# Moving the accumulations of the modulation vectors in a two-layer hybrid encoder from attention to the output projection and the feed-forward part

## The chip, the cores and the metric

The kernel runs on one core of a Trainium2 chip. The metric is the device time of one execution in microseconds (us), lower is better. Engines are named as in the profile: PE is TensorE (PEld its weight loads), DVE is VectorE, ACT is ScalarE, POOL is GpSimd, SP is SyncE, whose queue issues the transfers.

## The reference, cut to what matters

Two layers work on 256 tokens of 1024 channels in float32. Each layer has an attention part and a feed-forward part, and six modulation vectors of 1024 values that depend only on the conditioning vector `c` and on weights, and not on the tokens:

```
mod = silu(c) @ ada_w + ada_b                      # 1024 x 6144 weights in each layer
sh_m, sc_m, g_m, sh_f, sc_f, g_f = split(mod, 6)   # vectors 0 to 5

h = rms_norm(x, norm_mix_g) * (1 + sc_m) + sh_m    # vectors 1 and 0
proj = h @ w_in                                    # 1024 x 5024
... three attention branches, 4 + 4 + 8 heads ...
merged = sum of sigmoid(gate) * (branch @ w_branch)
x = x + g_m * (merged @ w_out)                     # vector 2

h = rms_norm(x, norm_ffn_g) * (1 + sc_f) + sh_f    # vectors 4 and 3
gate, up = split(h @ ffn_w_gate_up, 2)             # 1024 x 5632
x = x + g_f * ((silu(gate) * up) @ ffn_w_down)     # vector 5; 2816 x 1024
```

## The kernel before

**Items.** All large products are cut into items, in one list for both layers (`items`, 248 of them). An item is 256 rows by up to 512 columns of a weight (512 KB). `load_split` (L241) loads it from SP's queue into a buffer `raw` (five of them, `rawp`), ACT rounds it into `whi` (L187) and DVE takes the remainder into `wlo` (L188); there are seven pairs of these (`spl`). For each of the two blocks of 128 tokens PE then does six matmuls of 512 columns (three products for each 128 rows, L268 to L270). In the main loop the first block's `step` of an item is written down with the item and the second block's four items later (`LAG = 4`), except in the first twelve items, where both stand together. So a pair of `whi` and `wlo` is held from its split until the second block's matmuls.

In layer 0, items 0 to 17 are the first part of the input projection, 18 to 41 the gates, 42 to 49 the branch projections, 50 to 57 the output projection, 58 to 101 the gate and up part of the feed-forward part (`iF` is 58, `iD` is 102), 102 to 123 its down projection. Layer 1 follows with items 124 to 247; its gates are items 142 to 165. Attention has no items of its own: its pieces (scores, softmax, transposes, products) are set beside the items of the gates by `at(i, f)`, which runs `f` ahead of item i's load.

**Modulation vectors.** Vectors 1 and 0 of layer 0 are made ahead of everything (`first_sums`, `first_mod`). Each of the others is made in two halves of four units (`ada_units`, L143). A unit loads 256 x 512 of `ada_w` into one of the same five `raw` buffers from the same queue, and DVE multiplies each of its two slices by a value of silu(c) and adds it to `acc` (L138 for the first slice of a half, L140 for the other seven). After the fourth unit a half is summed over partitions: for vectors 0, 1, 3 and 4 by `col_mod` (four transposes on PE, a reduction and two or three small operations on DVE), for 2 and 5 by two matmuls and an addition. `spread` (L800) sets units at even distances beside a range of items. A unit stands ahead of the load of its item, so in SP's queue and in the ring of five buffers it goes first.

**Order.** The instructions of each engine are put in order at build time by a scheduler that follows the order in which they are written where operands allow; `manual_schedule` keeps PE's order inside a block as written. `later(k, fn)` writes `fn` k steps (a step is one block of an item) later. `na_bias` loads the bias table of the neighbourhood heads and adds the mask to it on DVE (L349). `post_g1` normalizes the low-rank parts; its late part `b_` (L379) transposes them and splits them for `w_uq` and `w_ukv` (items 16 and 17).

Of the kernel before, what the change touches and what calls it, by code (L numbers as in the profile page):

```python
# [12 lines left out]
ALU = mybir.AluOpType  # L13
AX = mybir.AxisListType

P = 128
# [5 lines left out]
W = 64  # L22
# [5 lines left out]
DC = 9  # L28
# [8 lines left out]
def encoder_kernel(ctx: ExitStack, tc: tile.TileContext, x, consts, cols, rows, ada_b, rpb, ada_w, w_in,  # L37
                   w_uq, w_ukv, w_na, w_mla, w_gqa, w_out, w_gu, w_dn, fng, out):
    nc = tc.nc
# [18 lines left out]
    def nm(s):  # L58
        uid[0] += 1
        return f"{s}_{uid[0]}"  # L60
# [4 lines left out]
    def t2(shape, dtype=F32):  # L65
        return tmp.tile(shape, dtype, tag="tm", name=nm("tm"))
# [4 lines left out]
    def tpb():  # L71
        return pstp.tile([P, 512], F32, tag="tp", name=nm("tp"))
# [16 lines left out]
    mask = con[:, o:o + 64]; o += 64  # L89
# [44 lines left out]
    def ada_acc(acc, raw, kc0, nk):  # L134
        for j in range(nk):
            kc = kc0 + j
            if kc == 0:
                nc.vector.tensor_scalar_mul(acc, raw[:, j, :], sc[:, 0:1])  # L138
            else:
                nc.vector.scalar_tensor_tensor(out=acc, in0=raw[:, j, :], scalar=sc[:, kc:kc + 1], in1=acc,  # L140
                                               op0=ALU.mult, op1=ALU.add)

    def ada_units(l, m, hf, row):  # L143
        st = {}

        def unit(u):
            def go():
                if u == 0:
                    st["acc"] = modp.tile([P, 512], F32, tag="acc", name=nm("acc"))
                raw = rawp.tile([P, 2, 512], F32, tag="raw", name=nm("raw"))  # L150
                c0 = m * D + hf * 512
                nc.sync.dma_start(raw, ada_w[l, u * 256:(u + 1) * 256, c0:c0 + 512].rearrange("(k p) n -> p k n", p=P))
                ada_acc(st["acc"], raw, 2 * u, 2)
                if u == 3:
                    fin()
            return go

        def fin():
            acc = st["acc"]
            if not row:  # L160
                later(DG, lambda: col_mod(l, m, hf * 4, 4, acc))
                return
            if hf == 0:
                mods[(l, m)] = modp.tile([P, D], F32, tag="G", name=nm("G"), bufs=1)
            bb = t2([P, 512])
            c0 = m * D + hf * 512
            nc.sync.dma_start(bb, ada_b[l, c0:c0 + 512].partition_broadcast(P))
            ah, al = t2([P, 512], F32R), t2([P, 512], F32R)
            split_to(ah, al, acc)

            def b_():
                ps = tpb()
                nc.tensor.matmul(ps, onesr, ah, start=True, stop=False)
                nc.tensor.matmul(ps, onesr, al, start=False, stop=True)
                nc.vector.tensor_tensor(out=mods[(l, m)][:, hf * 512:(hf + 1) * 512], in0=ps, in1=bb, op=ALU.add)

            later(DG, b_)

        return [unit(u) for u in range(4)]
# [6 lines left out]
    def split_to(hi_ap, lo_ap, src):  # L186
        nc.scalar.copy(hi_ap, src)  # L187
        nc.vector.tensor_tensor(out=lo_ap, in0=src, in1=hi_ap.bitcast(F32), op=ALU.subtract)  # L188
# [99 lines left out]
    def later(k, fn):  # L288
        deferred.append((cur[0] + k, fn))
# [8 lines left out]
    def at(i, fn):  # L298
        side.setdefault(i, []).append(fn)
# [9 lines left out]
    def layer(l):  # L309
# [3 lines left out]
        i0 = len(items)  # L313
# [24 lines left out]
        def na_bias():  # L338
            st["bias"] = []
            for t in range(NT):  # L340
                hk = t4([P, 16, W])
                for r in range(2):
                    base = rpb[l, 2 * t + r]
                    src = bass.AP(tensor=base.tensor, offset=base.offset, ap=[[1, W], [127, 16], [1, W]])
                    nc.sync.dma_start(hk[r * W:(r + 1) * W], src)
                b = t4([P, 16, W])
                rev = bass.AP(tensor=hk.tensor, offset=hk.offset + W - 1, ap=[list(hk.ap[0]), [W, 16], [-1, W]])
                for h in range(4):
                    nc.vector.tensor_tensor(out=b[:, 4 * h:4 * h + 4, :], in0=rev[:, 4 * h:4 * h + 4, :],  # L349
                                            in1=mask.unsqueeze(1).to_broadcast([P, 4, W]), op=ALU.add)  # L350
                st["bias"].append(b)

        def lazy(key, shape):
# [7 lines left out]
        def post_g1(t, ps):  # L361
            c = t2([P, 416])
            nc.scalar.copy(c, ps[:, 0:416])
            junk = t2([P, 512])
            s = sm(2)
            nc.scalar.activation(junk[:, 0:256], c[:, 0:256], AF.Square, scale=1.0 / 16.0, accum_out=s[:, 0:1])
            nc.scalar.activation(junk[:, 256:384], c[:, 256:384], AF.Square, scale=float(128.0 ** -0.5),
                                 accum_out=s[:, 1:2])
            ms = sm(2)
            nc.vector.tensor_scalar_add(ms, s, EPS)  # L370
            r = rstd_of(ms, 2)
            rw = st["rw"]
            cn = t2([P, 384])
            nc.vector.scalar_tensor_tensor(out=cn[:, 0:256], in0=c[:, 0:256], scalar=r[:, 0:1], in1=rw[:, 0:256],
                                           op0=ALU.mult, op1=ALU.mult)
            nc.vector.scalar_tensor_tensor(out=cn[:, 256:384], in0=c[:, 256:384], scalar=r[:, 1:2], in1=rw[:, 256:384],
                                           op0=ALU.mult, op1=ALU.mult)

            def b_():  # L379
                tpt = tpb()  # L380
                tv = tpt.rearrange("p (j q) -> p j q", j=4)
                for j in range(3):
                    nc.tensor.transpose(tv[:, j, :], cn[:, j * P:(j + 1) * P], ident)
                cT = t4([P, 2, 3, P], F32R)
                st.setdefault("cT", {})[t] = cT
                split_to(cT[:, 0], cT[:, 1], tv[:, 0:3, :])
                kr = c[:, 384:416]
                kpe = st["kpe"][:, t, :]
                ab = t2([P, 2, 32])
                a, b = ab[:, 0], ab[:, 1]  # L390
                nc.vector.tensor_tensor(out=a, in0=kr, in1=mlC[:, t, :], op=ALU.mult)
                for h in range(2):
                    nc.vector.tensor_tensor(out=b[:, h * 16:(h + 1) * 16], in0=kr[:, (1 - h) * 16:(2 - h) * 16],
                                            in1=mlS[:, t, h * 16:(h + 1) * 16], op=ALU.mult)
                nc.vector.tensor_tensor(out=kpe, in0=a, in1=b, op=ALU.add)

            later(DC, b_)

        def post_ga(t, ps):
            q = t2([P, 512])  # L400
# [138 lines left out]
        iB = len(items)  # L539
# [110 lines left out]

        flush.add(i0)
        at(i0 + (7 if l == 0 else 0), params)
        at(i0 + (12 if l == 0 else 8), na_bias)


        st["m"] = {}
# [35 lines left out]
        iO = len(items)  # L692
# [107 lines left out]
        def spread(units, a, b):  # L800
            n = len(units)
            for i, f in enumerate(units):
                at(a + (i * (b - a)) // n, f)

        spread([f for m, row in ((2, True), (4, False), (3, False)) for hf in range(2) for f in ada_units(l, m, hf, row)],
               i0 + 24, iB + 4)
        un = [f for hf in range(2) for f in ada_units(l, 5, hf, True)]
        if l + 1 < L:
            un += [f for m in (1, 0) for hf in range(2) for f in ada_units(l + 1, m, hf, False)]
        else:  # L810
            def load_fng():
                f = t4([P, D])
                nc.sync.dma_start(f, fng.partition_broadcast(P))
                state["fng"] = f
            at(iF + 30, load_fng)
# [5 lines left out]
    for l in range(L):  # L821
        layer(l)
    xT0 = {}

    def first_x():
        xT = act.tile([P, KC, S], F32, tag="lo", name=nm("xT"))
# [75 lines left out]
    for i, it in enumerate(items):  # L902
        if i in flush:
            while pend:
                step(1, pend.pop(0))
        if i == 0:
            raws = first_loads(0)
            first_x()
            first_mod(0, first_sums(0, raws))
        for f in side.get(i, ()):  # L910
            f()
        load_split(it)
        if i < 12:

            q1 = i // 3 + 1
            if i % 3 == 1 and q1 < 4:
                raws = first_loads(q1)
            with tc.manual_schedule(engines={mybir.EngineType.PE}):
                if i % 3 == 1 and q1 < 4:
                    four = first_sums(q1, raws)  # L920
                if i % 3 == 2 and q1 < 4:
                    first_mod(q1, four)
                step(0, i)
                step(1, i)
            continue
        if len(pend) >= LAG:
            step(1, pend.pop(0))
        step(0, i)
        pend.append(i)
# [71 lines left out]
```

## Time and profile before

| | |
|---|---|
| median of 3 runs | 822.5 us (822.18 to 823.59) |
| the profiled execution, its own time | 822.51 us |
| its span, from the first to the last instruction | 820.4 us |
| mean granted clock of TensorE | 0.991 |
| PE busy | 790.7 us (96%) |
| DVE busy | 598.8 us (73%) |
| ACT busy | 453.7 us (55%) |
| read from HBM | 185.44 MB, 227 GB/s over the span |

Busy times are unions of the instructions of an engine. PE's matmuls are pipelined, so short waits can hide in its busy time. The 2.1 us by which the execution is longer than its span lie around it.

### The profile page before, as it was taken

What the parts mean: (1) busy time and instruction counts of PE and PEld (TensorE: products, weight loads), DVE (VectorE), ACT (ScalarE), POOL (GpSimd) and SP (SyncE); (2) the same over time, 40 slices, a digit from 0 to 9 for tenths busy, and PEclk for the clock granted to TensorE, in tenths of its full rate; (3) what the DMA queues carried; (4) which work ended last, traced back from release to release, by engine and by line L of the source; (5) the groups of instructions that cost most, each with busy time, mean ns of one, the idle gap of its engine ahead of it and who ended that gap; (6) DMA issues with size and microseconds to landing.
All of it is one profiled execution on the core that took longest, in us unless ns stands there. A gap on an engine that the chain in (4) does not pass through costs nothing.

```text
span 820.4 us, 10803 instructions
## 1 busy us (share of the span) xinstructions
PE 790.7 (96%) x3776; PEld 633.4 (77%) x3776; DVE 598.8 (73%) x955; ACT 453.7 (55%) x788; POOL 25.8 (3%) x40
## 2 busy tenths in 40 slices
PE   5998999999999999999999999999999999999996
PEld 3786776788878888888878877777887888888884
DVE  3369898789777888875667699878978666665462
ACT  4365887644485444443466687774448544444441
POOL 1002100000000000000000020000000000000000
PEclk9999999999999999999999999999999999999998
DMA  9979488697667989886874668778765677876631
GB/s 315 359 245 273 131 293 252 198 311 227 194 180 241 322 294 306 276 264 190 210 213 137 180 192 279 222 230 283 250 198 182 219 233 223 259 226 184 182 103 52
DMA packets 113414, 187.20 MB, mean 228 GB/s; under 512 B 14672, under 2 KB 34256, under 8 KB 113360
## 3 DMA queue, kind: packets, MB, share of 16 engines
q1 hardware_dynamic: 113360, 186.51, 73.1%
q8 instruction: 30, 0.49, 0.3%
q14 instruction: 24, 0.20, 0.1%
HBM read 185.44 MB, written 1.05 MB: 227 GB/s over the span
## 4 chain that ended last, share of the span: by engine, by line
issue 49%; PE 31%; DVE 8%; DMA 6%; ACT 4%; POOL 1%; POOLq 0%; DVEq 0%; ACTq 0%
PE mm L268 8%; PE mm L270 8%; PE mm L269 8%; DMA raw<-in_ada_w_dram 6%; DVE wlo L188 2%; DVE acc L140 2%; PE tp L861 1%; POOL sm L108 1%; PE o L629 1%; ACT P L587 1%; ACT tm L218 1%; DVE sm L574 1%; PE tp L209 1%; PE tp L608 1%; PE tp L560 1%
## 5 line engine op out<-in xcount | busy, mean ns | idle before, releaser
L188 DVE TENSOR_TENSOR wlo<-raw,whi 128x1024 fp32r<-128x1024 f32 (+2 forms) x248 | 298.3, 1209 | 115.0 <-ACT whi L187 114.8
L187 ACT CAST whi<-raw 128x1024 fp32r<-128x1024 f32 (+2 forms) x248 | 256.9, 1041 | 221.6 <-PE mm L270 137.1
L268 PE MATMUL mm<-whi,hi 128*128 128x512 f32 (+1 forms) x784 | 314.0, 400 | 1.8 <-ACT hi L882 1.1
L270 PE MATMUL mm<-whi,lo 128*128 128x512 f32 (+1 forms) x784 | 307.1, 392 | 0.2
L269 PE MATMUL mm<-wlo,hi 128*128 128x512 f32 (+1 forms) x784 | 306.1, 390 | 0.5 <-DVE wlo L188 0.4
L268 PEld LDWEIGHTS mm<-whi,hi 128*128 128x128 f32 x784 | 148.1, 189 | 34.7 <-issue 5.7
L270 PEld LDWEIGHTS mm<-whi,lo 128*128 128x128 f32 x784 | 147.7, 188 | 32.8 <-DVE lo L188 1.8
L269 PEld LDWEIGHTS mm<-wlo,hi 128*128 128x128 f32 x784 | 148.3, 189 | 28.9 <-DVE wlo L188 1.7
L140 DVE SCALAR_TENSOR_TENSOR acc<-raw,sc,acc 128x512 f32<-128x512 f32 x140 | 104.9, 749 | 32.2 <-DMA raw<-in_ada_w_dram 30.5
L270 PE MATMUL mm<-whi,s 128*128 128x512 f32 (+1 forms) x188 | 73.3, 390 | 2.4 <-DVE s L188 2.4
L268 PE MATMUL mm<-whi,s 128*128 128x512 f32 (+1 forms) x188 | 74.2, 395 | 0.4 <-ACT s L187 0.4
L269 PE MATMUL mm<-wlo,s 128*128 128x512 f32 (+1 forms) x188 | 73.1, 389 | 0.0
L270 PEld LDWEIGHTS mm<-whi,s 128*128 128x128 f32 x188 | 35.4, 189 | 9.8 <-DVE s L188 2.6
L268 PEld LDWEIGHTS mm<-whi,s 128*128 128x128 f32 x188 | 35.3, 188 | 7.9 <-ACT s L187 0.9
L269 PEld LDWEIGHTS mm<-wlo,s 128*128 128x128 f32 x188 | 35.4, 188 | 6.8
L592 ACT ACTIVATE P<-P,sm 128x256 f32<-128x256 f32 x64 | 29.3, 509 | 5.7 <-DVE sm L590 5.6
L587 ACT ACTIVATE P<-tp,sm,rq 128x256 f32<-128x256 f32 x32 | 17.8, 561 | 15.9 <-DVE sm L584 15.8
L197 POOL TENSOR_SCALAR sm<-ss 128x1 f32<-128x1 f32 x10 | 4.0, 404 | 662.4 <-ACT tm L192 662.4
L218 ACT ACTIVATE tm<-tp,cm,cm 128x128 f32<-128x128 f32 x48 | 21.3, 472 | 6.2 <-PE tp L209 6.2
L108 POOL TENSOR_TENSOR sm<-sm,nhalf 128x1 f32<-128x1 f32 (+2 forms) x22 | 18.4, 835 | 127.1 <-DVE sm L370 65.2
L192 ACT ACTIVATE tm<-x_sb 128x512 f32<-128x512 f32 x20 | 12.6, 632 | 16.8 <-DVE x_sb L703 14.6
L733 DVE TENSOR_TENSOR tm<-tm,mm 128x512 f32<-128x512 f32 (+1 forms) x24 | 15.4, 640 | 8.7 <-PE mm L270 7.1
(157 smaller groups left out, 637.7 us busy)
## 6 DMA issues: line engine op xcount, KB each, us to landing
raw<-in_ada_w_dram SPq DMA_DIRECT2D x80, 512.0 KB, 4.8
raw<-in_w_gu_dram SPq DMA_DIRECT2D x80, 512.0 KB, 4.6
raw<-in_w_in_dram SPq DMA_DIRECT2D x64, 512.0 KB, 4.6
raw<-in_w_dn_dram SPq DMA_DIRECT2D x44, 512.0 KB, 4.8
s<-in_ada_w_dram SPq DMA_DIRECT2D x32, 256.0 KB, 6.7
raw<-in_w_out_dram SPq DMA_DIRECT2D x16, 512.0 KB, 4.9
raw<-in_w_in_dram SPq DMA_DIRECT2D x16, 256.0 KB, 5.0
raw<-in_w_gqa_dram SPq DMA_DIRECT2D x8, 512.0 KB, 5.6
```

Of the source, the lines that this page charges most:

```text
L108: nc.gpsimd.tensor_tensor(out=r, in0=ms, in1=nhalf[:, 0:n], op=ALU.pow)
L140: nc.vector.scalar_tensor_tensor(out=acc, in0=raw[:, j, :], scalar=sc[:, kc:kc + 1], in1=acc, op0=ALU.mult, op1=ALU.add)
L187: nc.scalar.copy(hi_ap, src)
L188: nc.vector.tensor_tensor(out=lo_ap, in0=src, in1=hi_ap.bitcast(F32), op=ALU.subtract)
L192: nc.scalar.activation(junk, x_sb[:, t, hf * 512:(hf + 1) * 512], AF.Square, scale=1.0 / 32.0, accum_out=ss[:, hf:hf + 1])
L218: nc.scalar.activation(fv[:, j, :], xT[:, j, :], AF.Identity, scale=A[:, kc:kc + 1], bias=B[:, kc:kc + 1])
L268: nc.tensor.matmul(ps[t][:, 0:n], lhs(t, 0, kc), hi[:, j, 0:n], start=first, stop=False)
L269: nc.tensor.matmul(ps[t][:, 0:n], lhs(t, 0, kc), lo[:, j, 0:n], start=False, stop=False)
L270: nc.tensor.matmul(ps[t][:, 0:n], lhs(t, 1, kc), hi[:, j, 0:n], start=False, stop=last)
L587: nc.scalar.activation(pt[:, t, :], src[:, t, :], AF.Exp, bias=nb[:, t:t + 1], scale=scale[t], accum_out=rs[:, t:t + 1])
L592: nc.scalar.activation(pt[:, t, :], pt[:, t, :], AF.Copy, scale=rc[:, t:t + 1])
L733: nc.vector.tensor_tensor(out=hd[:, 0:n], in0=sgv, in1=up, op=ALU.mult)
```

## The change

Of the units, layer 0's vectors 2, 4 and 3 (24 units) are spread over items 24 to 53 and no longer over 24 to 45. Layer 1 keeps only vector 2 (8 units) beside its attention; its vectors 4 and 3 (16 units) go to the feed-forward part of layer 0, whose 34 items 68 to 101 so get 40 units in place of 24, in the order 5, 1, 0, 4, 3. Four smaller edits come with it. The mask is added by one instruction in place of four. `na_bias` of layer 0 stands at item 11 in place of 12. The late part of `post_g1` in layer 0 comes 6 steps after it in place of 9. In the first twelve items each block's PE instructions are put behind the last PE instruction written before them (an edge in PE's own order; nothing waits for a result).

```diff
-                for h in range(4):
-                    nc.vector.tensor_tensor(out=b[:, 4 * h:4 * h + 4, :], in0=rev[:, 4 * h:4 * h + 4, :],
-                                            in1=mask.unsqueeze(1).to_broadcast([P, 4, W]), op=ALU.add)
+                nc.vector.tensor_tensor(out=b, in0=rev, in1=mask.unsqueeze(1).to_broadcast([P, 16, W]), op=ALU.add)
...
-            later(DC, b_)
+            later(6 if l == 0 else DC, b_)
...
-        at(i0 + (12 if l == 0 else 8), na_bias)
+        at(i0 + (11 if l == 0 else 8), na_bias)
...
-        spread([f for m, row in ((2, True), (4, False), (3, False)) for hf in range(2) for f in ada_units(l, m, hf, row)],
-               i0 + 24, iB + 4)
+        ms = ((2, True), (4, False), (3, False)) if l == 0 else ((2, True),)
+        spread([f for m, row in ms for hf in range(2) for f in ada_units(l, m, hf, row)], i0 + 24, iO + 4 if l == 0 else iB + 4)
         un = [f for hf in range(2) for f in ada_units(l, 5, hf, True)]
         if l + 1 < L:
-            un += [f for m in (1, 0) for hf in range(2) for f in ada_units(l + 1, m, hf, False)]
+            un += [f for m in (1, 0, 4, 3) for hf in range(2) for f in ada_units(l + 1, m, hf, False)]
...
+    def last_pe():
+        return next(i for i in reversed(nc.cur_bb.bb.instructions) if i.engine == mybir.EngineType.PE)
...
-            with tc.manual_schedule(engines={mybir.EngineType.PE}):
+            with tc.issue_after(last_pe()), tc.manual_schedule(engines={mybir.EngineType.PE}):
```

## Rows read from the trace of the kernel before

**Rows 1.** The page: busy time, share and instructions of each engine.

```profile
PE 790.7 (96%) x3776; PEld 633.4 (77%) x3776; DVE 598.8 (73%) x955; ACT 453.7 (55%) x788; POOL 25.8 (3%) x40
```

**Rows 2.** Stretches of 20 us: length, busy of each engine, clock, DMA share, GB/s.

```profile
0.00:20.00 20.00, 9.94 (x45) 6.59 (x46) 5.84 (x18) 9.85 (x19) 2.25 (x8) 0.92 0.95 314
...
60.00:80.00 20.00, 16.93 (x79) 13.36 (x78) 18.67 (x50) 12.67 (x23) 5.07 (x5) 0.96 1.00 262
80.00:100.00 20.00, 19.88 (x103) 14.37 (x101) 17.16 (x47) 17.43 (x47) 2.24 (x2) 0.96 0.47 129
...
800.00:820.00 20.00, 12.57 (x56) 10.09 (x54) 4.27 (x6) 2.89 (x6) 1.72 (x4) 0.89 0.14 53
```

**Rows 3.** PE's waits from 60 to 100 us: total, times, longest.

```profile
PE mm L270 <- DVE s L188: 2.4, 1, 2.4
PE mm L268 <- ACT s L187: 0.4, 1, 0.4
```

**Rows 4.** DVE's timeline around that wait: start, duration, instruction.

```profile
62.24 0.35 DVE L376 SCALAR_TENSOR_TENSOR tm<-tm,sm,rw 128x128 f32<-128x128 f32 x1
...
75.20 1.42 DVE L349 TENSOR_TENSOR s<-s,con 128x256 f32<-128x256 f32 x4
76.54 1.01 DVE L188 TENSOR_TENSOR s<-tp,s 128x384 fp32r<-128x384 f32 x2
```

**Rows 5.** PE's timeline: the second block's transposes of `post_g1`.

```profile
66.42 0.49 PE L383 MATMUL tp<-con,tm 128*128 128x128 f32 x3
```

**Rows 6.** Stages of layer 0, columns as in rows 2.

```profile
97.00:160.00 63.00, 61.48 (x319) 45.61 (x318) 51.42 (x89) 47.13 (x107) 0.00 (x0) 1.00 0.78 251
...
182.00:216.00 34.00, 34.00 (x163) 28.17 (x162) 31.91 (x43) 15.20 (x17) 0.00 (x0) 1.00 0.71 220
216.00:234.00 18.00, 17.05 (x80) 13.95 (x79) 12.58 (x15) 10.82 (x19) 1.09 (x2) 1.00 0.67 201
...
258.00:346.00 88.00, 88.00 (x411) 72.84 (x410) 73.46 (x95) 39.08 (x46) 0.00 (x0) 1.00 0.91 305
...
358.00:424.00 66.00, 65.17 (x299) 53.76 (x297) 38.57 (x47) 29.72 (x37) 1.14 (x2) 1.00 0.76 209
```

**Rows 7.** Stages of layer 1: attention, and the gate and up part.

```profile
460.00:560.00 100.00, 97.82 (x516) 75.00 (x515) 85.69 (x159) 74.63 (x163) 5.75 (x5) 1.00 0.74 225
...
650.00:740.00 90.00, 90.00 (x414) 74.45 (x413) 58.43 (x63) 43.13 (x50) 0.00 (x0) 1.00 0.76 236
```

**Rows 8.** ACT's longest waits, 258 to 346 us (layer 0, gate and up).

```profile
ACT whi L187 <- DMA raw<-in_w_gu_dram: 33.8, 19, 3.1
ACT whi L187 <- PE mm L270: 6.0, 4, 3.1
```

**Rows 9.** ACT's longest wait, 650 to 740 us (layer 1, gate and up).

```profile
ACT whi L187 <- PE mm L270: 32.5, 21, 2.1
```

**Rows 10.** All of DVE's waits, 258 to 346 us.

```profile
DVE acc L140 <- DMA raw<-in_ada_w_dram: 11.0, 10, 1.6
DVE acc L138 <- DMA raw<-in_ada_w_dram: 3.0, 3, 1.3
```

**Rows 11.** PEld's only wait, 258 to 358 us.

```profile
PEld mm L269 <- DVE wlo L188: 0.3, 1, 0.3
```

**Rows 12.** The tile `acc`: durations in ns, least, median, most.

```profile
L140 DVE SCALAR_TENSOR_TENSOR acc<-raw,sc,acc x140: 728/751/754, 92.5 to 718.7; 128x512 f32<-128x512 f32 x140
...
L138 DVE TENSOR_SCALAR acc<-raw,sc x20: 474/482/489, 86.7 to 682.4; 128x512 f32<-128x512 f32 x20
```

**Rows 13.** DVE's groups by shape, 255 to 350 us: busy us, mean ns.

```profile
L188 DVE TENSOR_TENSOR wlo<-raw,whi 128x1024 fp32r<-128x1024 f32 x33 | 40.1, 1220 | 0.0
...
L124 DVE TENSOR_REDUCE sm<-tp 128x4 f32<-128x512 f32 x3 | 2.1, 685 | 0.0
```

**Rows 14.** Transfers, 258 to 346 us: GB/s in 40 slices, bytes, unit loads.

```profile
GB/s 246 358 358 361 285 355 338 337 294 273 245 398 356 352 344 334 294 337 317 283 221 173 296 279 383 299 222 371 358 287 294 279 263 237 306 281 385 275 274 256
DMA packets 14741, 26.85 MB, mean 305 GB/s; under 512 B 877, under 2 KB 2447, under 8 KB 14735
...
raw<-in_ada_w_dram SPq DMA_DIRECT2D x20, 512.0 KB, 5.2
```

## The prediction

> **What bounds the kernel now.** I began with the page's busy times: PE is busy for 790.7 of 820.4 us, no other engine above 599 [rows 1]. So the kernel is a stream of matmuls, and a change can give back only what PE idles, about 30 us, or add idle time where something fails to feed it. The profiled execution took 822.51 us, which is the median (822.5), so sums against it need no correction; its 2.1 us around the span I leave alone. A difference under 0.2% (1.6 us) I count as no change.
>
> Next I looked for the idle time in the windows of 20 us. Ten of the first 20 us (first loads) and 7.4 us of the last 20 (last norm and store) lie outside what is edited [rows 2]. Inside, from 60 to 80 us, 3.1 us are missing, and the clock falls to 0.96 in that window and in the next [rows 2]. The waits name the cause: 2.4 us for the remainder split of the low-rank transposes, 0.4 for its rounding [rows 3]. Attention hides very little: PE is busy 61.48 of 63 us in layer 0 and 97.82 of 100 in layer 1 [rows 6, 7]. That is the whole visible price of what is moved away: 1.5 and 2.2 us.
>
> Then I read the place that the work is moved to. From 258 to 346 us (items about 69 to 100) PE is busy for 88 of 88 us, so there is nothing to win; the question is what feeds it. DVE is busy 73.46 of 88 us, the transfers run at 305 GB/s [rows 6, 14]. The telling view is ACT's waits, two stages side by side. In layer 1's gate and up part, where 8 units stand beside the same number of items, ACT waits for PE to free a weight buffer: the feed is ahead and all buffers are full [rows 9]. In layer 0, with 24 units, ACT waits 33.8 us for weights to land and only 6.0 for PE [rows 8]: the feed is behind, and PE was just not starved. One weight load in that stretch does wait for its DVE half, 0.3 us [rows 11]. So this stage already sits at the limit of its feed, and the change adds 16 units to it.
>
> **The change part by part.**
>
> *Attention.* Layer 0 goes from a unit at 24/22 = 1.09 per item to 24/30 = 0.8; layer 1 from 1.09 to 8/22 = 0.36. The most to be had is PE's idle time there, 1.5 + 2.2 = 3.7 us; the least is nothing, since softmax waits on chains of its own. I take a third of the first and three quarters of the second: **-2.2 us** (0 to -3.7).
>
> *The low-rank parts.* The late part of `post_g1` moves three steps of six matmuls ahead. Today the second block's transposes start at 66.42 us [rows 5], and their source is complete at 62.24 + 0.35 = 62.59 [rows 4], so about 4 us are there to be used. DVE's part of the split, at 76.54, stands behind one of the two groups of four mask additions, 1.42 us, at 75.20 [rows 4]; both come earlier. At best this returns 2.4 + 0.4 us and the dip of the clock, 0.04 x 20 us in each of two windows = 1.6 us, together 4.4 us [rows 2, 3]. DVE is busy 18.67 of those 20 us [rows 2], so the wait may come back at the next thing it is late with, the rotary products of the queries. I take **-3 us** (0 to -4.4).
>
> *The mask in one instruction, one item earlier.* 1024 elements in one go: the nearest row is `wlo` of the same size, 1.22 us [rows 13], against 1.42 for four [rows 4]. Four times 0.2 us of DVE time, covered by PE's matmuls outside the stretch already counted: nothing of its own. Its four table loads pass one weight load in SP's queue, at a place where the five buffers cycle anyway: nothing, at worst one split late in the stretch above.
>
> *The order edge.* In the timeline up to item 11 PE's blocks already follow each other as written, so an edge that demands this order changes nothing there: 0, with a bound of the 0.4 us by which PE's short waits are seen [rows 3].
>
> *The output projection.* Six units land beside items 46 to 52, where one addition stood before. A unit costs DVE (7 x 0.751 + 0.482)/4 = 1.435 us [rows 12], so 8.6 - 0.75 = 7.9 us come on top of 31.91 in a stretch of 34 [rows 6]: 5.8 us more than it holds. From 216 to 234 us DVE idles 18 - 12.58 = 5.4 us [rows 6], and split weights already waiting for PE cover part of the delay; but the branch sums that PE's transposes wait for stand in the same DVE order. Between nothing and 5.8 us I take the middle: **+3 us**.
>
> *Layer 0's gate and up part.* In this stretch 20 unit loads were issued [rows 14]; at 40 units for 24 that is 33.3, so 13.3 more. Three quantities give the cost.
> DVE: 13.3 x 1.435 = 19.1 us, and four more halves to be summed, about 0.69 us each with small additions [rows 13], some 3 us: 73.5 + 22.1 = 95.6 us of work in 88. With DVE never idle that is +7.6 us. At the present share (73.46/88 = 83.5%) it is 114.5, +26.5 us. DVE's idle time here is 11.0 + 3.0 us of waits for unit loads to land [rows 10]; if half of them stay, 95.6 + 7 = 102.6, +14.6 us.
> Transfers: 26.85 + 13.3 x 0.524 = 33.8 MB. At the mean of 305 GB/s that takes 111 us, +23 us; at the best slice of the row, 398 GB/s, 85 us, no limit at all [rows 14].
> Reserve: weights split ahead would hide the first microseconds, but the wait of 0.3 us says that the stretch ends with none left [rows 11].
> The ring of five buffers ties the two together: a unit holds a buffer for its transfer (5.2 us, [rows 14]) and its turn on DVE, and the weights behind it in SP's queue wait for that buffer, then ACT, then PE. I take **+15 us** (+7.6 to +26.5).
>
> Whether transfers alone would bind is where the Trainium skill can be weighed. The slices show up to 398 GB/s for 2.2 us, but the mean is 305 at a share of 0.91 [rows 6, 14]. The page DMA: Bandwidth & Descriptors (Specifications) gives a limit of about 358 GB/s for a core's share of HBM; by it, an estimate, 33.8 MB take 94 us, +6 us. That speaks against the change too, and lies below DVE's term. The slices above it show that it is no hard limit here.
>
> *Cover.* Layer 1's attention loses its units to a place where nothing covers them; the down projection behind it, with 66 - 38.57 = 27 us of idle DVE [rows 6], gets none, because the units stand ahead of items 68 to 101.
>
> **Sum.** -2.2 - 3 + 3 + 15 = +12.8 us: 822.5 + 12.8 = **835 us**. All ends at their best: 822.5 - 3.7 - 4.4 + 0 + 7.6 = 822.0; at their worst, 822.5 + 5.8 + 26.5 = 855.
>
> **The rivals.**
> *The feed has room (faster).* The 14 us that DVE idles in the stretch are waits for transfers that a denser queue would have ready, and what DVE still lacks, 7.6 us, slips behind item 101 as far as buffers allow: five loads, at most 5 x 1.435 = 7 us of unit work. Then the stage costs 0 to 2 us and the output projection little, and the gains stand: 822.5 - 5.2 + 1 = 818 us. For it: DVE would have to work at 100%, and transfers at some 385 GB/s, which single slices reach [rows 14]. Against it: ACT's waits [rows 8], and a ring in which a late weight can't be overtaken. It decides from a cost of this stage below about 4 us. The page Perfetto Trace Analysis (Roofline) would allow it, giving some 435 GB/s as the ceiling of a single core's transfers; no slice here comes near that. Chance 0.17.
> *A draw.* DVE fully busy (+7.6), everything in front of it at its best (-8.1): 822 us. Chance 0.07.
> *Every late weight also stalls a chain.* DVE late by several us delays the hidden products and their transposes too, waits of PE lower its clock as between 60 and 100 us [rows 2], and the output projection pays its 5.8: above 850 us. Chance 0.10.
> *The forecast*, 824 to 850 us: 0.66.
>
> **How the numbers follow.** Slower is 0.66 + 0.10 = 0.76, same 0.07, faster 0.17. The range leaves out about 0.07 below, the faster case at its best, and 0.10 above: 816 to 850. The likeliest case's own range is 824 to 850.
>
> **What would show it.** Right: between about 258 and 360 us PE shows idle time, its waits name `wlo` and `whi` in the gate and up part, DVE is above 90% there, and the stage from items 68 to 101 is 10 to 20 us longer; ACT still waits for weights to land. The 2.4 us wait near 75 us is gone or under 1 us, and the clock of 60 to 100 us is nearer 1.00. Layer 1's attention is about 2 us shorter. Wrong: PE busy throughout that stage with DVE near 97% would be the first rival; a wait of PE for `post_g1`'s transposes near 62 us, or for the branch sums near 200 us above 6 us, would mean that a small edit or the output projection was mis-sized.

## The result, and the profile after

The changed kernel takes **833.76 us** (median of 5 runs, 832.54 to 836.02) against 822.5 (5 runs, 822.18 to 824.03): 1.0131 times the time before, 95% interval 1.0109 to 1.0153. It is slower, near the forecast of 835. The profiled execution took 833.52 us with a span of 831.5, 11.0 us more than the one of before.

The page's busy times, which answer to [rows 1]:

```profile
PE 797.1 (96%) x3776; PEld 632.8 (76%) x3776; DVE 600.6 (72%) x943; ACT 454.1 (55%) x788; POOL 25.5 (3%) x40
```

PE does the same 3776 matmuls and shows 6.4 us more busy time, so part of its waiting stands in its busy time and the busy share can't locate the loss; the number of matmuls in a stretch can. The stages, columns as in [rows 6, 7]:

```profile
97.00:160.00 63.00, 61.39 (x315) 46.13 (x314) 50.65 (x87) 48.00 (x109) 0.00 (x0) 0.97 0.72 229
182.00:216.00 34.00, 34.00 (x162) 27.70 (x161) 33.48 (x50) 12.99 (x16) 0.00 (x0) 1.00 0.69 220
216.00:234.00 18.00, 17.05 (x82) 13.97 (x82) 16.47 (x21) 11.68 (x19) 1.09 (x2) 1.00 0.93 310
258.00:346.00 88.00, 85.82 (x390) 67.12 (x389) 80.77 (x113) 33.81 (x41) 0.00 (x0) 1.00 0.93 317
...
460.00:560.00 100.00, 98.55 (x517) 76.60 (x516) 73.49 (x150) 74.33 (x161) 6.36 (x6) 1.00 0.60 179
```

Between 258 and 346 us PE gets through 390 matmuls in place of 411, although only 2.2 us of idle time show: a matmul has 85.82/390 = 0.220 us of busy time in place of 88/411 = 0.214. DVE rises from 73.46 to 80.77 us. The output projection (182 to 234 us) carries its new units with PE as busy as before. The waits of that stretch, which answer to [rows 8, 10, 11]:

```profile
ACT whi L187 <- DMA raw<-in_w_gu_dram: 41.8, 20, 4.2
PEld mm L269 <- DVE wlo L188: 5.8, 12, 1.1
ACT whi L187 <- PE mm L270: 4.3, 1, 4.3
DVE wlo L188 <- ACT whi L187: 3.8, 5, 2.2
...
DVE acc L140 <- DMA raw<-in_ada_w_dram: 2.2, 1, 2.2
...
PE mm L269 <- DVE wlo L188: 1.3, 2, 0.8
```

PE's side now waits for `wlo`, 12 times in its weight loads where it did once before. But DVE in turn waits for ACT's `whi`, and ACT waits 41.8 us for weights to land. The load, in turn, waits for a buffer. These are the longest waits of SP's queue in the same stretch (L152 issues the load of a unit, L247 that of an item):

```profile
SPq L152 <- DVE wlo L188: 18.8, 13, 2.5
SPq L247 <- DVE acc L140: 14.4, 14, 1.7
SPq L247 <- DVE wlo L188: 14.1, 7, 3.7
SPq L152 <- DVE acc L140: 10.4, 10, 1.7
```

With two smaller rows (L138), SP's queue waits 62.9 of 88 us for DVE to be done with a buffer (56.8 in the kernel before). So the chain is a circle: ACT and DVE wait for a load to land, and the next load waits for the buffer that DVE gives back. The transfers of that stretch, which answer to [rows 14]:

```profile
DMA packets 14451, 27.88 MB, mean 317 GB/s; under 512 B 864, under 2 KB 864, under 8 KB 14446
...
raw<-in_ada_w_dram SPq DMA_DIRECT2D x30, 512.0 KB, 5.3
```

30 unit loads in place of 20, but only 1.03 MB more than before: weights of the items give way.

A plain ruler for the stages is given by the transposes of the first block (L209) at the norms: into layer 0's feed-forward part, into layer 1, into layer 1's feed-forward part. PE's timeline of before, then of after:

```profile
231.72 1.07 PE L209 MATMUL tp<-con,tm 128*128 128x128 f32 x8 [0.95 <-DVE tm L202]
...
423.12 1.07 PE L209 MATMUL tp<-con,tm 128*128 128x128 f32 x8 [0.83 <-DVE tm L202]
...
622.65 1.07 PE L209 MATMUL tp<-con,tm 128*128 128x128 f32 x8 [0.95 <-DVE tm L202]
```

```profile
232.36 1.06 PE L209 MATMUL tp<-con,tm 128*128 128x128 f32 x8 [0.95 <-DVE tm L202]
...
436.68 1.06 PE L209 MATMUL tp<-con,tm 128*128 128x128 f32 x8 [1.11 <-DVE tm L202]
...
633.71 1.07 PE L209 MATMUL tp<-con,tm 128*128 128x128 f32 x8 [0.95 <-DVE tm L202]
```

Up to the first nothing is won or lost (+0.6). Layer 0's feed-forward part takes 204.3 us in place of 191.4 (+12.9), layer 1 up to its own norm 197.0 in place of 199.5 (-2.5), the rest is equal to 0.1.

For a finer division I counted PE's matmuls in the trace in their written order, which gives the start of each item's first matmul. The table shows by how many us each stage of each profiled version is longer than in the profile of before; the feed-forward part is cut at item 88, where the first 24 of the 40 units end (68 + 34 x 24/40 = 88.4).

```
items              0-36   36-68  68-88  88-108 108-130 130-172
after              -0.1   +0.8   +6.3   +4.9   +2.1   -2.9
ffn_alone          +0.6    0.0   +5.8   +5.7    0.0   -3.0
out_alone           0.0   +1.5   +0.7   +1.2    0.0   -0.6
small_edits        -0.1   +0.1   +0.3   +1.3   +2.2   +0.3
mask_in_four       +1.5    0.0   +0.4   +1.5   +0.1   -0.5
units_no_add       -1.6   +1.4   +7.6   +3.7   +2.0   -3.1
units_no_load      +1.8   +1.7   +6.2   +0.5   +2.2   -3.2
ring6              +0.4   +1.4   +1.9   +1.9   +1.2   -2.2
no_add_ring6       +0.5   +1.0   +2.1   +1.9   +1.2   -2.0
before_ring4       +4.5   +2.0   +2.3   +3.3   +0.1   +3.1
down_proj          +0.9    0.0   +0.7   +6.7   +9.9   -3.1
down_and_input     -0.1    0.0    0.0   +5.4  +10.1   -2.4
input_l1           +0.1    0.0   -0.1   -0.1   +3.3   -1.3
```

Versions that are alike in a stage differ by up to 1.8 us between items 68 and 108, 1.2 in the last column, 0.9 in the other two and 3.4 in the first; smaller differences are not read. Items 68 to 108 are up to 1.9 us longer even in versions that change nothing there (`out_alone` and `mask_in_four` +1.9, `small_edits` +1.6). One execution of `input_l1` took 995.87 us at a granted clock of 0.752; the ratio below leaves it out, and without it the median is 825.91 us.

### The profile page after: what moved, and what is told of

It reads as the page before. It is cut to its first block, busy times and chain, and to the rows that moved or that the text cites. A ratio compares the mean times of both kernels' runs of the same rounds, so it can differ in the third digit from the quotient of the medians.

```text
span 831.5 us, 10794 instructions
## 1 busy us (share of the span) xinstructions
PE 797.1 (96%) x3776; PEld 632.8 (76%) x3776; DVE 600.6 (72%) x943; ACT 454.1 (55%) x788; POOL 25.5 (3%) x40
## 4 chain that ended last, share of the span: by engine, by line
issue 47%; PE 39%; DVE 4%; ACT 4%; DMA 4%; POOL 1%; SPq 0%; POOLq 0%; DVEq 0%; ACTq 0%
PE mm L268 10%; PE mm L270 10%; PE mm L269 10%; DMA raw<-in_ada_w_dram 2%; PE o L627 2%; DVE wlo L188 2%; PE tp L558 1%; PE tp L606 1%; PE tp L862 1%; ACT tm L218 1%; ACT P L585 1%; DMA con<-in_consts_dram 1%; PE tp L209 1%; DMA raw<-in_w_in_dram 1%; POOL sm L108 1%
## 5 line engine op out<-in xcount | busy, mean ns | idle before, releaser
L532 ACT ACTIVATE s<-mm 128x512 f32<-128x512 f32 x24 | 14.4, 599 | 14.1 <-PE mm L270 14.1
```

Source lines behind the costliest of these rows:

```text
L532: nc.scalar.activation(st["gate"][gi][:, t, :], ps, AF.Tanh, scale=0.5)
```

## The experiments

Ratios, with their 95% intervals, stand against runs of the kernel before on the same chip, whose medians were 823.4 to 824.3 us; they are worked out over the runs and need not equal the ratio of two medians.

**Which edit costs it.** Three kernels take the change apart. `ffn_alone` is before with only layer 1's 16 units moved into the feed-forward part of layer 0:

```diff
-            un += [f for m in (1, 0) for hf in range(2) for f in ada_units(l + 1, m, hf, False)]
+            un += [f for m in (1, 0, 4, 3) for hf in range(2) for f in ada_units(l + 1, m, hf, False)]
```

> The kernel before with one edit: layer 1's vectors 4 and 3 (16 units) moved into layer 0's gate and up part. If the feed of that part is the cause: 10 to 15 us lost there, 2 to 3 us back in layer 1's attention, 830 to 834 us. If the small edits or the output projection carry the loss, this stays within 822 to 825 us.

831.97 us, 1.0086 [1.0066, 1.0106]. `out_alone` only stretches layer 0's own units to the output projection (`iO + 4 if l == 0 else iB + 4`):

> The kernel before with one edit: layer 0's units spread on to item 53. The forecast gave +3 us (0 to 5.8) for the output projection and -0.5 for attention: 825 us. The rival, that split weights waiting for PE and the idle DVE behind item 54 cover it: 822 to 823.5 us.

826.94 us, 1.0041 [1.0023, 1.0058]. `small_edits` is the changed kernel with both `spread` edits undone:

> The kernel after with the units put back where they were before, so the four small edits alone. The forecast gave them -3 us (0 to -4.4): 819.5 us. The rival, from the profile after: the 2.4 us wait is gone but other waits before item 18 have taken its place, so nothing is left: 822 to 823.5 us.

825.95 us, 1.0017 [0.9999, 1.0035]. So the 16 units carry two thirds of the loss, 0.86 of 1.31%, and in the table `ffn_alone` shows +11.5 in items 68 to 108, as the full change does (+11.2). `out_alone` costs 0.41%, which is 3.4 us (1.9 to 4.8): it fits the forecast, not the rival. `small_edits` can't be told from no change, as its rival said. None of the three parts gains.

**What of a unit costs it.** A unit is a load of 512 KB and two additions on DVE. `units_no_add` cuts the additions of the 16 moved units to 8 of 512 columns and keeps their loads:

```diff
-                ada_acc(st["acc"], raw, 2 * u, 2)
+                if l == 1 and m in (3, 4):
+                    if u == 0:
+                        nc.vector.memset(st["acc"], 0.5)
+                    ada_acc(st["acc"][:, 0:8], raw[:, :, 0:8], 2 * u, 2)
+                else:
+                    ada_acc(st["acc"], raw, 2 * u, 2)
```

> The kernel after, with the 16 moved units' additions cut from 512 columns to 8: their loads stay in the queue and in the ring of five, but DVE has hardly any of their work (vectors 4 and 3 of layer 1 are left out of the result but for their bias). If DVE's time is the limit of the gate and up part, nearly all of its loss goes: 822 to 824 us. If the transfers and the ring are, nearly all of it stays: 830 us or more. A mix shows as 825 to 829.

832.54 us, 1.0113 [1.0079, 1.0146]. `units_no_load` keeps the additions and takes the loads away: the 16 units add a tile that is there anyway.

```diff
+                if l == 1 and m in (3, 4):
+                    ada_acc(st["acc"], x_sb[:, :, 0:512], 2 * u, 2)
+                    if u == 3:
+                        fin()
+                    return
```

> The kernel after, with the 16 moved units adding up a resident tile in place of loaded weights: DVE's work stays in full, the transfers and the turns in the ring go (vectors 4 and 3 of layer 1 are thereby wrong). If DVE's time is the limit, the loss stays: 830 us or more. If transfers and the ring are, it goes: 820 to 824 us.

831.02 us, 1.0088 [1.0055, 1.0121]. Read by their totals, the two seem to say that loads and additions each cost nearly everything. The total misleads, because both edits touch only the last 16 of the 40 units. The first 24 (vectors 5, 1 and 0) are the same as before the change, but squeezed from 34 items into 20, and they cost 6 to 8 us in all versions with five buffers. The edits must be read in items 88 to 108 alone. The window of 60 us in that part, of after, `units_no_add` and `units_no_load`:

```profile
325.00:385.00 60.00, 58.28 (x264) 44.83 (x263) 55.82 (x75) 27.32 (x32) 0.00 (x0) 1.00 0.96 325
```

```profile
325.00:385.00 60.00, 58.79 (x270) 46.02 (x269) 42.65 (x77) 28.21 (x34) 0.00 (x0) 1.00 0.96 328
```

```profile
325.00:385.00 60.00, 60.00 (x286) 49.35 (x285) 56.76 (x80) 28.89 (x34) 0.00 (x0) 1.00 0.64 210
```

Without the additions DVE has 13 us less to do and PE is still starved (+3.7 in the table, not clear of the +4.9 of after). Without the loads DVE is busy 95% of the time, more than in the changed kernel, and PE is busy for 60.00 of 60 us (+0.5). In these items the loads are the price and the additions of the 16 units are free. The first 24 units, squeezed into items 68 to 88, were not taken apart in this way.

**Is it the ring?** A sixth `raw` buffer, with all units as in the change (room for it is made by four in place of six buffers of another pool, which serves attention and the last norm):

```diff
-    rawp = ctx.enter_context(tc.tile_pool(name="rawp", bufs=5))
+    rawp = ctx.enter_context(tc.tile_pool(name="rawp", bufs=6))
...
-    ppl = ctx.enter_context(tc.tile_pool(name="ppl", bufs=6))
+    ppl = ctx.enter_context(tc.tile_pool(name="ppl", bufs=4))
```

> The kernel after with six load buffers in place of five; to make room, attention has four buffers for its probabilities in place of six, which may cost time in the two attentions, so what counts is the gate and up part of layer 0 (items 68 to 101) by its own length. If the ring ties the feed, that part is at least 4 us shorter than after. If DVE is fully busy or the transfers are at their end, it keeps its length within 2 us.

827.03 us, 1.0041 [1.002, 1.0061]. The loss of items 68 to 108 falls from 11.2 to 3.8 us. In the first half of the part, of after and of `ring6`:

```profile
262.00:322.00 60.00, 57.82 (x259) 44.69 (x258) 54.74 (x76) 23.05 (x28) 0.00 (x0) 1.00 0.92 315
```

```profile
262.00:322.00 60.00, 59.19 (x277) 48.55 (x276) 57.56 (x80) 25.38 (x30) 0.00 (x0) 1.00 0.96 339
```

With one more buffer DVE does more work (57.56 of 60 us) and PE still does 18 matmuls more. A DVE that had been the limit at 54.74 could not have allowed that. `no_add_ring6` joins this edit with that of `units_no_add`:

> The kernel after with the 16 moved units' additions cut to 8 columns and with six load buffers (attention's probabilities again have four). With five buffers the cut of the additions gave nothing back. If the buffers are the limit, items 68 to 101 now lose at most 3 us against before. If the bytes themselves are, as many as in after, they lose 8 us or more.

827.46 us, 1.0035 [1.0013, 1.0056]: nothing more is won, +4.0 in the part against +3.8. So the additions of the 16 units are free with six buffers, too. What is left lies between the two cases expected (at most 3 us, 8 or more). `before_ring4` takes a buffer from the kernel before and adds no work at all (`rawp` with `bufs=4`):

> The kernel before with four load buffers in place of five and nothing else: no more DVE work and no more bytes anywhere. If the number of buffers is what ties the feed of layer 0's gate and up part, and before ran at that limit, this part (items 68 to 101) gets at least 8 us longer with 24 units, as it does with 40 units and five buffers, while layer 1's, with 8 units, stays within 1 us. If DVE's time or the transfers are the limit, it keeps its length within 2 us.

837.35 us, 1.0159 [1.0123, 1.0195]. In items 68 to 108 it loses 5.6 us, less than the 8 us expected of that part but more than the 2 us that DVE or the transfers as the limit would have left; layer 1's gate and up part (items 182 to 225) keeps its length to 0.1 us, as expected. The rest lies in the first 36 items (+4.5), in items 36 to 68 (+2.0) and in layer 1's attention (+3.1). The loads issued from 259 to 355 us, of `before_ring4`, after and `ring6` (a pair of 256 KB fills one buffer):

```profile
raw<-in_w_gu_dram SPq DMA_DIRECT2D x28, 512.0 KB, 4.7
raw<-in_ada_w_dram SPq DMA_DIRECT2D x21, 512.0 KB, 4.8
raw<-in_w_gu_dram SPq DMA_DIRECT2D x4, 256.0 KB, 4.3
```

```profile
raw<-in_ada_w_dram SPq DMA_DIRECT2D x31, 512.0 KB, 5.3
raw<-in_w_gu_dram SPq DMA_DIRECT2D x25, 512.0 KB, 5.3
...
raw<-in_w_gu_dram SPq DMA_DIRECT2D x2, 256.0 KB, 4.9
```

```profile
raw<-in_ada_w_dram SPq DMA_DIRECT2D x33, 512.0 KB, 5.5
raw<-in_w_gu_dram SPq DMA_DIRECT2D x25, 512.0 KB, 5.4
raw<-in_w_gu_dram SPq DMA_DIRECT2D x6, 256.0 KB, 4.9
```

51, 57 and 61 buffers filled in 96 us with four, five and six of them. The first is the kernel before with its 24 units; with five buffers that kernel fills 55 in the same 96 us. If all buffers were always in use, a buffer would be held 4 x 96/51 = 7.5, 5 x 96/57 = 8.4 and 6 x 96/61 = 9.4 us, of which the transfer of an item or a unit takes 4.7 to 5.5; the rest is the time until it is issued and until ACT and DVE are done with the buffer. The changed kernel asks for more loads than five buffers turn over, and it gets one only when one comes free.

**Do idle engines cover the units elsewhere?** The down projection had 27 us of idle DVE [rows 6]. `down_proj` puts the 16 units there and leaves the gate and up part alone:

```diff
+        if l + 1 < L:
+            spread([f for m in (4, 3) for hf in range(2) for f in ada_units(l + 1, m, hf, False)], iD, iE)
```

> The kernel before, with the same 16 units of layer 1's vectors 4 and 3 moved into the down projection of layer 0 (items 102 to 123), where DVE idles 27 of 66 us, and the gate and up part left at 24 units. If the loss is the feed of the gate and up part, the gain of layer 1's attention (2 to 3 us) stays and the units (16 x 1.435 + 3 = 26 us of DVE) just fit: 819.5 to 823 us. If 16 units cost a fixed sum wherever they are put beside the weights, 828 us or more.

837.37 us, 1.0152 [1.013, 1.0174], no better than the change. That is the second case expected, though the sum is not a fixed one: 16.6 us in items 88 to 130 for the same 16 units. One window of 20 us, then the waits from 356 to 440 us:

```profile
380.00:400.00 20.00, 18.43 (x85) 14.44 (x84) 14.12 (x22) 7.18 (x9) 0.00 (x0) 1.00 0.78 261
```

```profile
ACT whi L187 <- DMA raw<-in_w_dn_dram: 34.8, 14, 5.0
DVE acc L140 <- DMA raw<-in_ada_w_dram: 13.2, 11, 2.7
...
PE mm L269 <- DVE wlo L188: 6.2, 6, 3.0
```

DVE is busy 71% of that window, the transfers 78%, ACT 36%: nothing is full, and PE is starved. From 356 to 440 us as a whole these are 77, 85 and 39%; only in the last 20 us do the transfers reach a share of 1.00 (at 292 GB/s). ACT and DVE wait for loads to land, and SP's queue waits 46.8 of the 84 us for the splits and additions of DVE to give a buffer back, as in a ring that turns too slowly. That one more buffer would help here was not tried. Thinner, over items 102 to 141 (`iD, iE + 18`), it stays bad:

> The kernel before, with the 16 units of layer 1's vectors 4 and 3 spread over layer 0's down projection and the first 18 items of layer 1 (items 102 to 141), 0.4 per item. If density is what costs, this loses nothing there and keeps layer 1's attention gain: 819.5 to 821.5 us, faster than both kernels. If the units disturb the norm between the layers, 823 us or more.

835.79 us, 1.0146 [1.0118, 1.0175]. `input_l1` keeps layer 1's 24 units in layer 1 and starts them at its item 6, where the input projection runs (`i0 + (24 if l == 0 else 6)`):

> The kernel before with one edit: layer 1's 24 units start at its item 6 in place of 24, so that they spread over its input projection and gates (0.6 per item in place of 1.1), a place between a norm and attention where loads run at 186 GB/s or less and DVE idles 8 of 24 us. If thinning out attention is worth 2 to 3 us and five buffers carry 0.6 units per item there: 819.5 to 821.5 us, faster than both kernels. If density near 0.6 costs time here too, as in the down projection: 823 us or more.

826.23 us, 1.0024 [1.0004, 1.0044]. It returns 1.3 us in layer 1's attention and loses 3.3 at the norm in front of it, where the clock is 0.91 from 425 to 445 us. No version beat the kernel before.

**The small edits.** `small_edits` and after lose 2 us at the norm between the layers (items 108 to 130), `ffn_alone` doesn't. `mask_in_four` is `small_edits` with the mask added in four instructions again:

> The four small edits without the mask's: it stays four instructions. In small_edits and in after, PE's order at the norm between the layers differs from before, three waits stand close together and the clock halves for 3 us, about 2 us in all; ffn_alone, which has the four instructions, keeps before's order there. If the mask in one instruction is the cause, that stretch is back to before's length and the whole is about 2 us under small_edits. If another small edit is, it stays.

824.34 us, 0.9999 [0.998, 1.0019], and +0.1 in that column. PE's timeline of after there:

```profile
436.68 1.06 PE L209 MATMUL tp<-con,tm 128*128 128x128 f32 x8 [1.11 <-DVE tm L202]
438.39 0.46 PE L268 MATMUL mm<-whi,hi 128*128 128x416 f32 x1 [0.65 <-ACT hi L187]
438.69 0.35 PE L269 MATMUL mm<-wlo,hi 128*128 128x416 f32 x1
439.46 0.71 PE L270 MATMUL mm<-whi,lo 128*128 128x416 f32 x1 [0.42 <-DVE lo L188]
439.97 0.55 PE L268 MATMUL mm<-whi,hi 128*128 128x416 f32 x1
```

and of `mask_in_four`:

```profile
426.54 1.07 PE L209 MATMUL tp<-con,tm 128*128 128x128 f32 x8 [0.83 <-DVE tm L202]
427.36 0.48 PE L268 MATMUL mm<-whi,s 128*128 128x512 f32 x1
...
428.84 0.35 PE L268 MATMUL mm<-whi,hi 128*128 128x416 f32 x1
```

With four short instructions six matmuls of the down projection (`s`) stand behind the transposes and cover the rounding of `hi`. With the long one the order made at build time puts them in front; PE waits three times, the granted clock falls to 0.53 (439.9 to 442.9 us), and its next matmuls of 416 columns take 0.55 us in place of 0.35.

## Why the prediction was right, step by step

- **Layer 0's gate and up part**, taken as +15 (7.6 to 26.5): +11.2 up to item 108, of which +9.9 stand in items 68 to 101. The place, the sign and the ring as what ties the terms were right. The reasoning for the size was not: it was priced by DVE's work, with "DVE never idle is +7.6" as the floor. `units_no_load` shows DVE 95% busy beside a PE that loses 0.5 us in its half of the part, and `ring6` costs 3.8 us in all. Part of DVE's excess slips behind item 101, as the first rival said it would, though not as additions: in `ring6` the last of them starts at 363.3 us and item 102 at 363.7, but from there to item 108 DVE is busy 14.58 of 17.5 us where it was 10.50 of 17.2. The price is that of the loads: 16 more of them at 11.2/16 = 0.7 us each on the mean, and 3.8/16 = 0.24 with a sixth buffer. A cost below about 4 us, from which that rival would have decided, came with the sixth buffer alone.
- **DVE above 90% there**, as predicted (80.77 of 88 us), but as a link, not as the limit: its waits show it behind ACT, ACT behind the loads, and the loads behind the buffers that DVE holds.
- **Transfers**, between 0 and +23: not a limit of their own with five buffers, since `ring6` moves 339 GB/s where after moves 315. With six their share is 0.94 to 0.96; that what is left is theirs was not tried, and DVE is 96% busy in the first half, too (57.56 of 60 us). Of these 3.8 us, up to 1.9 also show in versions that change nothing in these items.
  The page DMA: Bandwidth & Descriptors (Specifications) of the Trainium skill gives about 358 GB/s, by which the prediction estimated +6; the 339 GB/s that `ring6` sustained over 60 us at a share of 0.96 lie 5% below that. The page Perfetto Trace Analysis (Roofline) of the Trainium skill gives some 435 GB/s, which would have allowed the faster rival; the fastest slice of 2.2 us of after between 258 and 346 us reached 410, and 339 over 60 us is the most that the windows above show.
- **The low-rank parts**, -3, and **layer 0's attention**, the -0.5 within the -2.2: together -0.1. This step failed. The wait of 2.4 us [rows 3] is gone as foreseen, and in this execution the clock is back at 1.00 where it was 0.96 [rows 2], as the windows of 20 us of after show:

```profile
60.00:80.00 20.00, 17.69 (x85) 14.34 (x85) 18.40 (x48) 14.09 (x24) 4.00 (x4) 1.00 0.62 203
80.00:100.00 20.00, 19.55 (x98) 13.84 (x97) 17.60 (x41) 17.21 (x45) 2.34 (x3) 1.00 0.59 172
```

  But that is not the rule: of the seven versions with these edits only `units_no_add` has 1.00 there, too; the five others have 0.91 from 60 to 80 us. In after it is 0.97 later, from 97 to 160 us, as it is in `out_alone`, which lacks these edits. And PE's timeline has other waits from 58 us on:

```profile
58.90 0.52 PE L381 MATMUL tp<-con,tm 128*128 128x128 f32 x3 [0.56 <-DVE tm L372]
59.69 0.50 PE L268 MATMUL o<-whi,hi 128*128 128x512 f32 x1 [0.26 <-ACT whi L187]
61.35 0.50 PE L269 MATMUL o<-wlo,hi 128*128 128x512 f32 x1 [1.16 <-DVE wlo L188]
...
69.57 0.50 PE L269 MATMUL mm<-wlo,hi 128*128 128x512 f32 x1 [1.15 <-DVE wlo L188]
```

  0.56 + 0.26 + 1.16 + 1.15 = 3.1 us. The second block's transposes went from 66.42 us [rows 5] to 58.90, their source only from 62.59 [rows 4] to 59.02: the 4 us between them are used up, and PE waits for the source. DVE's mask addition, one item earlier, runs right before the `wlo` that PE waits for at 61.35 us:

```profile
58.94 1.22 DVE L348 TENSOR_TENSOR s<-s,con 128x1024 f32<-128x1024 f32 x1
60.07 2.36 DVE L188 TENSOR_TENSOR wlo<-raw,whi 128x1024 fp32r<-128x1024 f32 x2
```

  That this addition causes the 1.16 us is argued from the order, not shown. Its being one instruction is not the cause: `mask_in_four` has the same two waits for `wlo` at 1.36 and 1.58 us. The other three small edits were not taken apart. The seven versions with these edits stand at -1.6 to +1.8 us at item 36, 0.3 on the mean, like the five with five buffers that lack them (0.3).
- **The output projection**, +3 (0 to 5.8): +0.8 in its column, +1.5 in `out_alone`. DVE fills up as computed (33.48 of 34 us) while PE stays as busy as before, so in this execution the term was too large; that weights split ahead covered the rest is argued. By all its runs `out_alone` costs 3.4 us (1.9 to 4.8), with attention's -0.5 near what was forecast, and its profiled execution (825.18 us) is one of its fastest. So how large the term is stays open.
- **The mask in one instruction**, priced at nothing: right for layer 0, wrong for layer 1, where it cost 2.1 us. The prediction looked for it beside layer 0's low-rank stretch alone; layer 1's copy stands at the norm between the layers.
- **Layer 1's attention**, -1.7 within the -2.2: -2.9, of which 2.2 were visible as PE's idle time [rows 7].
- **The third rival**, chains that stall and a clock that falls with them: not in that stretch, where the clock stays at 1.00; a small case of it came at the norm between the layers.
- **The sum**: -0.1 + 0.8 + 11.2 + 2.1 - 2.9 = +11.1, where the profiled executions differ by 11.0. The forecast +12.8 was that near by luck, because errors of both signs cancelled: gains of 3.4 us that didn't come, against two terms that were 6.0 us too large; 2.1 us that were not foreseen and 1.2 more in layer 1's attention make the rest.

Open: why the down projection loses more than the gate and up part for the same 16 loads (6.7 + 9.9 = 16.6 us in items 88 to 130; its clock is 0.93 from 360 to 380 us and 0.91 from 440 to 460, as an estimate (0.07 + 0.09) x 20 = some 3 us of it), and how much of the remaining 3.8 us of `ring6` is the transfers', DVE's or scatter.

## What to carry to other kernels

Here work that takes a slot of a shared ring of load buffers was priced by the slot, not by the time of the engine that consumes it: look for the stage where the ring has slots to spare (the compute side of it waits for PE, as in [rows 9]), not for the stage where the consuming engine idles. That a stage with slots to spare takes such loads for nothing was not tried. An idle engine beside a starved PE, with transfers below their best, points to such a ring; one more buffer is the cheap test, as `ring6` was for the gate and up part. When an experiment removes half of a cost, read it in the items it touches, not in the total.

## What was not expected of the hardware

- After three waits of 1.11, 0.65 and 0.42 us within 4 us, eight matmuls of 416 columns took 0.51 to 0.55 us in place of 0.35, from 439.97 to 442.9 us, at a granted clock of 0.53; in `mask_in_four`, with a wait of 0.83 us alone ahead of them, they kept 0.35 at a granted clock of 1.00 (426 to 434 us).
- With five buffers the changed kernel already takes the transfers to 315 to 325 GB/s at a share of 0.92 to 0.96, and a sixth buffer adds 24 GB/s in the first half of the part and nothing in the second (324); but 7% more loads (61 for 57 in 96 us) went with two thirds of the stall (11.2 us down to 3.8).
